# GLA's output projection keeps all its weights on chip, the FFN's norm rows take Ln and Exp, and two steps move in the projections' order

## The chip, the cores and the metric

The kernel runs on one core of one Trainium2 chip. The core has TensorE (PE in the profile, its weight loads PEld), VectorE (DVE), ScalarE (ACT), GpSimd (POOL) and SyncE (SP, which here issues nearly all DMAs). The metric is the device time of one execution in microseconds: 2878.23 us as the median of three runs before the change.

## The reference

One step of an encoder trunk of two layers. 1056 tokens (1024 of a new stream, 32 of a running one), width 1024, all in float32:

```
layer 0: x += Retention(RMSNorm(x));  x += ConvFFN(RMSNorm(x))
layer 1: x += GLA(RMSNorm(x));        x += ConvFFN(RMSNorm(x))
y = RMSNorm(x)

rmsnorm(x, g) = x * rsqrt(mean(x*x) + 1e-6) * g
retention:  ... -> (silu(g) * groupnorm(o)) @ w_out      w_out 2048 x 1024
gla:        ... -> (silu(r) * rmsnorm_head(o)) @ w_out   w_out 1024 x 1024
conv_ffn:   u = h @ w_up (1024 x 5632), causal convolution of width 3,
            silu(gate) * value, @ w_down (2816 x 1024)
```

It also returns the recurrent states of both mixers and the last rows of each convolution.

## The kernel before

**Products.** Activations are held with the width on the 128 partitions and the tokens on the free axis. A float32 product is made of three matmuls: each operand is split into a high half (a cast on ScalarE) and a low half (a subtraction on VectorE, `raw - hi`), and high x high, high x low and low x high are added up in PSUM. A weight of 128 x 1024 is loaded by `load_w` (L99): a DMA of 512 KB into one of three raw slots (L94), the cast and the subtraction of L104 into two of ten "w" tiles (L97) or, for kept weights, into a room of its own ("kw", three pairs).

**The output projections.** The class `Down` (L1211) does retention's (16 k tiles, weights w_ro), GLA's (8 k tiles, w_go) and the last k tiles of each FFN's down projection (6). The first two are named d1 in the code. The tokens are cut into parts: four of 264 for d1, three of 384, 384 and 288 for the FFN. In each part the loop runs over the k tiles; `load` (L1235) brings the weight, unless it is kept from an earlier part, and the part's 264 or 384 columns of the input h, in a raw slot hr of which there are four, and splits them into hh and hl (L1248, L1249; the page calls them XB where they lie in that buffer), of which there are eight each. Each k tile has 8 x 3 matmuls into the eight banks of PSUM (pd, L1273 to L1275). The matmuls of the last k tile go bank by bank, and behind each bank comes its eviction: VectorE adds the residual (L1662 in d1, L1728 in layer 0's down projection), ScalarE squares the result (L138), VectorE and GpSimd add up the squares (L149, L197), and SyncE stores it (L1665).

In parts 1 to 3 the first k tiles are done on seven banks, so that the eighth is free for the norm of the part before: after `hold` k tiles (4 in d1, 3 in the FFN) TensorE sums the squares over the partitions (pn, L201) and `rms_row` (L207 to L212) makes the row 1/rms: mean and epsilon (rm), Sqrt on ScalarE, a reciprocal on VectorE, and one Newton step of three VectorE operations. Then come the eighth bank's matmuls of the steps so far. The work put off to later steps (`done`, `x_sums`) scales the eight tiles by that row (L1678) and makes the sums and splits that the FFN needs (L1339, L1340, L1344). Before the change GLA's d1 keeps k tiles 2 to 4 and loads the other five again in every part; retention's keeps 3 to 5 of 16.

**The FFN's up projection** works in pairs of 128-column blocks by seven products in place of eight. `pair_weights` (L292) makes the seven weights of a pair: two raw loads, rg and rv (L294, L295, in the same three raw slots), and the halves wgh/wgl, wv, wsh/wsl, wth/wtl (L300 to L311, in w tiles). ScalarE and VectorE take the results out of PSUM (pu; L1527 and L1523). The norm of the last part, its scaling and splits are done while the first pair's first products run.

**What sets the order.** The tile framework puts the instructions of each engine into one fixed row when the kernel is built; each engine works through its row in order and waits there on semaphores. Since `run` calls load, matmul and eviction in a certain sequence, the sequence of the code, and the slots of the rooms, decide the rows. `run_tails` (L1201) does four last transposes of retention (pt, from `on`, L831) and their storing, at a chosen place in the following projection.

**Around it.** Layer 1's GLA ends in a gate stage (1966 to 2046 us), which computes silu(r) and multiplies (L1643, L1644); its last weight loads overlap with the first of the projection. The projection follows to 2150 us, then the FFN.

## Time and profile before

| | |
|---|---|
| median of 3 runs | 2878.23 us (2876.97 to 2879.57) |
| profiled execution | 2871.2 us |
| its span | 2869.3 us |
| mean granted TensorE clock | 0.993 |
| TensorE busy | 2791.4 us, 20954 matmuls |
| VectorE busy | 2145.1 us |
| ScalarE busy | 1332.3 us |
| GpSimd busy | 277.8 us |
| retention's projection, layer 0 | 718 to 910 us |
| GLA's projection, layer 1 | 2046 to 2150 us |

The page gives one profiled execution; its time is compared with itself after the change, and the medians with each other. A line such as "PE pd L1274 <- DVE XB L1249: 2.0, 1, 2.0" says that matmuls of line 1274 into pd waited 2.0 us in all, once, 2.0 us the longest, for VectorE's line 1249. A row of the timeline has its start, its length (matmuls are pipelined, so their lengths overlap and the distance of two starts is what one costs), engine, line, operation and tiles, and in brackets the idle time of the engine in front of it with what ended that. PEclk is the granted clock as a share of full speed.

### The profile page before, as it was taken

How to read it: one execution, taken by the hardware profiler on the slowest of the kernel's cores; microseconds unless marked ns; L12 is line 12 of the kernel's file. 1: busy time of each engine (PE TensorE's matmuls, PEld its weight loads, DVE VectorE, ACT ScalarE, POOL GpSimd, SP SyncE). 2: the span in 40 equal slices, each digit the busy share in tenths (PEclk: the TensorE clock that was granted, in tenths of full speed). 3: DMA queues.
4: the chain of work that ended last, by engine and by line, in shares of the span. 5: the costliest groups of instructions: out<-in, count | busy, mean ns of one | idle time of the engine just before them, and what ended most of it. 6: DMA issues, size and time to landing. Idle time of an engine off the chain costs nothing.

```text
span 2869.3 us, 52602 instructions
## 1 busy us (share of the span) xinstructions
PE 2791.4 (97%) x20954; PEld 2687.3 (94%) x20954; DVE 2145.1 (75%) x3529; ACT 1332.3 (46%) x2401; POOL 277.8 (10%) x516
## 2 busy tenths in 40 slices
PE   8999999999999999999999999999998999999998
PEld 8999988788999999999999889999998999999997
DVE  7777777777678887878775577774498788878756
ACT  8433344444444544445443455553254444445434
POOL 1000000000000111111000232220011111110001
PEclk9999999999999999999999999999999999999999
DMA  6333377664765223333867201114642233428663
GB/s 219 106 124 103 128 262 239 199 192 154 260 210 166 82 75 128 121 128 113 286 205 246 90 27 46 51 44 153 222 155 70 75 110 123 143 75 271 210 231 115
DMA packets 234486, 427.22 MB, mean 149 GB/s; under 512 B 27616, under 2 KB 146016, under 8 KB 233216
## 3 DMA queue, kind: packets, MB, share of 16 engines
q1 hardware_dynamic: 233696, 423.27, 44.4%
q8 instruction: 164, 2.69, 0.4%
q14 instruction: 82, 0.67, 0.1%
q10 hardware_dynamic: 544, 0.59, 0.1%
HBM read 299.94 MB, written 123.85 MB: 148 GB/s over the span
## 4 chain that ended last, share of the span: by engine, by line
PE 80%; DVE 9%; DMA 4%; ACT 3%; issue 2%; POOL 1%; SPq 0%; DVEq 0%; ACTq 0%; POOLq 0%
PE pu L333 16%; PE pu L328 16%; PE pu L332 16%; PE pd L1274 3%; PE pd L1275 3%; PE pd L1273 3%; PE psv L233 2%; PE psv L232 2%; PE psv L231 2%; PE pj L124 1%; PE pj L126 1%; PE pj L125 1%; PE pg L124 1%; PE pg L125 1%; PE pg L126 1%
## 5 line engine op out<-in xcount | busy, mean ns | idle before, releaser
L104 DVE TENSOR_TENSOR wlo<-raw,whi 128x1024 fp32r<-128x1024 f32 x161 | 201.3, 1253 | 97.3 <-ACT whi L104 46.0
L1527 ACT COPY AR<-pu 128x264 f32<-128x264 f32 x264 | 99.0, 375 | 303.0 <-PE pu L333 300.3
L104 ACT CAST whi<-raw 128x1024 fp32r<-128x1024 f32 x161 | 167.8, 1047 | 118.4 <-DMA raw<-w_ro 26.7
L333 PE MATMUL pu<-XA,wgl 128*128 128x264 f32 x752 | 213.8, 284 | 0.0
L328 PE MATMUL pu<-XA,wgh 128*128 128x264 f32 x752 | 213.3, 284 | 0.0
L332 PE MATMUL pu<-XA,wgh 128*128 128x264 f32 x752 | 213.2, 283 | 0.0
L1274 PE MATMUL pd<-XB,whi 128*128 128x264 f32 x552 | 158.2, 288 | 2.2 <-DVE XB L1249 2.2
L1549 DVE SCALAR_TENSOR_TENSOR AR<-AR,cw 128x1058 f32<-128x1058 f32 x88 | 115.9, 1318 | 58.5 <-ACT AR L1548 55.9
L1275 PE MATMUL pd<-XB,wlo 128*128 128x264 f32 x552 | 158.3, 288 | 0.0
L1273 PE MATMUL pd<-XB,whi 128*128 128x264 f32 x552 | 154.0, 287 | 0.0
L328 PE MATMUL pu<-XA,wsh 128*128 128x264 f32 x520 | 148.7, 286 | 1.7 <-DVE AR L1523 1.0
L333 PE MATMUL pu<-XA,wsl 128*128 128x264 f32 x520 | 148.6, 286 | 0.8 <-DVE wsl L301 0.8
L332 PE MATMUL pu<-XA,wsh 128*128 128x264 f32 x520 | 147.8, 284 | 0.0
L301 DVE TENSOR_TENSOR wtl<-rv,wth 128x1024 fp32r<-128x1024 f32 x58 | 71.0, 1225 | 101.6 <-ACT wth L300 99.6
L1523 DVE TENSOR_TENSOR AR<-AR,pu 128x264 f32<-128x264 f32 (+2 forms) x440 | 144.6, 368 | 0.0
L328 PEld LDWEIGHTS pu<-XA,wgh 128*128 128x128 f32 x752 | 141.6, 188 | 0.0
L332 PEld LDWEIGHTS pu<-XA,wgh 128*128 128x128 f32 x752 | 141.5, 188 | 0.0
L333 PEld LDWEIGHTS pu<-XA,wgl 128*128 128x128 f32 x752 | 141.4, 188 | 0.0
L328 PE MATMUL pu<-XA,whi 128*128 128x264 f32 x448 | 127.5, 285 | 3.8 <-ACT XA L1418 3.0
L333 PE MATMUL pu<-XA,wlo 128*128 128x264 f32 x448 | 127.3, 286 | 1.5 <-DVE wlo L104 1.5
L332 PE MATMUL pu<-XA,whi 128*128 128x264 f32 x448 | 127.0, 285 | 0.2
L328 PE MATMUL pu<-XA,wth 128*128 128x264 f32 x408 | 116.3, 285 | 0.1
(478 smaller groups left out, 10547.1 us busy)
## 6 DMA issues: line engine op xcount, KB each, us to landing
raw<-w_ro SPq DMA_DIRECT2D x52, 512.0 KB, 4.8
rg<-w_up SPq DMA_DIRECT2D x44, 512.0 KB, 3.6
rv<-w_up SPq DMA_DIRECT2D x44, 512.0 KB, 3.5
scr_h<-AR SPq DMA_DIRECT2D x44, 512.0 KB, 2.7
AR<-scr_x SPq DMA_DIRECT2D x32, 528.0 KB, 4.9
scr_x<-AR SPq DMA_DIRECT2D x32, 528.0 KB, 3.6
raw<-scr_w SPq DMA_DIRECT2D x32, 512.0 KB, 5.2
AR<-scr_h SPq DMA_DIRECT2D x28, 528.0 KB, 4.8
```

The costliest lines, as they stand in the source:

```text
L104: ins = S.copy(hi, raw), V.tensor_tensor(lo, raw, hi.bitcast(F32), op=ALU.subtract)
L124: PE.matmul(ps, hi[:, k], rh, start=kt == 0, stop=False)
L301: V.tensor_tensor(l_, src, h.bitcast(F32), op=ALU.subtract)
L328: mm = PE.matmul(ps, wh[:, k], x[:, 0, kt], start=m in (1, 2, 4, 5) and kt == 0, stop=False, skip_group_check=True)
L332: PE.matmul(ps, wh[:, k], x[:, 1, kt], start=False, stop=False, skip_group_check=True)
L333: mm = PE.matmul(ps, wl[:, k], x[:, 0, kt], start=False, stop=kt == 3, skip_group_check=True)
L1273: PE.matmul(o, w[0][:, k], h[0][:, :n], start=i == 0, stop=False)
L1274: PE.matmul(o, w[0][:, k], h[1][:, :n], start=False, stop=False)
L1275: self.last_mm = PE.matmul(o, w[1][:, k], h[0][:, :n], start=False, stop=i == nk - 1)
L1523: V.tensor_tensor(u[:, d:d + n], t[:, o:o + n], b[:, o:o + n], op=op)
L1527: S.copy(t, b)
L1549: V.scalar_tensor_tensor(cj, uj[:, 1:T + 3], cw[:, nt, 1:2], cj, op0=ALU.mult, op1=ALU.add)
```

## The change

- `rms_row`, for the rows of both d1 (not for the final norm): ScalarE makes Ln of the mean and then Exp of -0.5 times it, which is 1/rms, in place of Sqrt on ScalarE and the reciprocal on VectorE. The table set that holds both is loaded ahead, once a layer: in layer 0 behind retention's last Sqrt, in layer 1 behind the gate's last silu. The Newton step stays.
- GLA's d1 keeps all eight weights: k tiles 2, 3 and 4 in the room "kw", and 0, 1, 5, 6 and 7 in the ten w tiles (`ring`). Its last part takes the k tiles of the ring first.
- `load` issues the DMA of the input h ahead of that of the weight, and `run` calls the load of the next part's first k tile before the last k tile's matmuls and evictions. This holds for all of `Down`.
- `run_tails` is called in part 1, after its second k tile, in place of part 0.

```diff
-        S.activation(t_, m_, AF.Sqrt)
-        V.reciprocal(r_, t_)
+        if logs[0]:
+            for ins in (S.activation(t_, m_, AF.Ln), S.activation(r_, t_, AF.Exp, scale=-0.5)):
+                order(ins, logs[0])
+        else:
+            S.activation(t_, m_, AF.Sqrt)
+            V.reciprocal(r_, t_)
...
-        def __init__(self, nk, wsrc, hsrc, chunks, res, sm, keep, hold, narrow=0):
-            self.narrow = narrow
+        def __init__(self, nk, wsrc, hsrc, chunks, res, sm, keep, hold, narrow=0, ring=()):
+            self.narrow, self.ring = narrow, list(ring)
...
+            hr = self.room("hr")[:, :n]
+            nc.sync.dma_start(hr, self.hsrc(kt)[:, c0:c0 + n])
             if kt not in self.keep:
                 w = load_w(self.wsrc(kt))
             else:
                 if kt not in self.kept:
-                    self.kept[kt] = load_w(self.wsrc(kt), self.room("kw"))
+                    self.kept[kt] = load_w(self.wsrc(kt), None if kt in self.ring else self.room("kw"))
                 w = self.kept[kt]
-            hr = self.room("hr")[:, :n]
-            nc.sync.dma_start(hr, self.hsrc(kt)[:, c0:c0 + n])
...
                     kts = list(keep) + [k for k in kts if k not in keep]
+                    if c == len(self.chunks) - 1:
+                        kts = self.ring + [k for k in kts if k not in self.ring]
...
                     self.load(c, kt)
+                    if i == nk - 1 and c + 1 < len(self.chunks):
+                        self.load(c + 1, (self.ring if c + 2 == len(self.chunks) and self.ring else list(keep))[0])
...
-                        if c == 0 and i == self.narrow:
-                            run_tails(sm)
...
                         for nt in range(KT - 1):
                             mm(i, nt)
+                        if c == 1 and i == 1:
+                            run_tails(sm)
...
             d1 = d1r if l == 0 else Down(ntile, lambda k: io[wo][k], lambda k: scr[k], CQ, scr_x if l else io["xT"], sm,
-                      range(2, 5), 4)
+                      range(8), 4, ring=(0, 1, 5, 6, 7))
             d1.sm = sm
+            logs[0] = S.preload_act_table_set("natural_log_exp_and_others")
+            order(logs[0], last_r[0])
```

The new lines shift the numbers: in the rows of the changed kernel L208 and L215 to L217 are the norm's row, L210 its Ln and Exp, L1253 and L1254 the split of h, L1245 its DMA, L1280 to L1282 the matmuls into pd, L1671 and L1740 the evictions, L299 and L300 the raw loads of `pair_weights`.

More of the change, by code (lines that the diff above doesn't have):

```diff
@@ L158, in trunk_kernel @@
     last_r = [None]
+    logs = [None]
     def rms_a(ss, c, ps, again=False, after=None):
@@ L811, in chunk @@
                             op0=ALU.mult, op1=ALU.add)
-            S.activation(ab[:L, 1:2], ab[:L, 0:1], AF.Sqrt)
+            last_r[0] = S.activation(ab[:L, 1:2], ab[:L, 0:1], AF.Sqrt)
             V.reciprocal(ab[:L, 1:2], ab[:L, 1:2])
@@ L1642, in second @@
             run_tails(sm)
-            S.activation(sg, sg, AF.Silu)
+            last_r[0] = S.activation(sg, sg, AF.Silu)
             V.scalar_tensor_tensor(sg, o, gn[:, f:f + 1], sg, op0=ALU.mult, op1=ALU.mult)
@@ L1716, in second @@
         if last:
+            logs[0] = None
             with pool("db") as dp:
```

## The prediction

> **What bounds the kernel now.** I read the page's busy times and chain first, then the windows of the stage that the change touches most, GLA's output projection in layer 1 (2046 to 2150 us) and the start of the FFN behind it, then what TensorE waited for there.

> ```profile
> PE 2791.4 (97%) x20954; PEld 2687.3 (94%) x20954; DVE 2145.1 (75%) x3529; ACT 1332.3 (46%) x2401; POOL 277.8 (10%) x516
> PE 80%; DVE 9%; DMA 4%; ACT 3%; issue 2%; POOL 1%; SPq 0%; DVEq 0%; ACTq 0%; POOLq 0%
> ```

> TensorE is busy 97% of the span, and the change removes no matmul. So only its waits, and stretches at a lower granted clock, can be won. The windows of the stage give, in order: PE, PEld, DVE, ACT, POOL busy, the granted clock, the DMA share and GB/s.

> ```profile
> 2069.00:2092.00 23.00, 23.00 (x190) 22.93 (x189) 16.63 (x30) 11.22 (x21) 3.56 (x6) 1.00 0.50 158
> 2092.00:2119.00 27.00, 26.28 (x211) 25.68 (x210) 25.82 (x45) 14.17 (x27) 4.50 (x6) 1.00 0.56 184
> 2119.00:2150.00 31.00, 27.12 (x194) 26.64 (x195) 29.72 (x48) 14.44 (x23) 8.23 (x10) 0.90 0.46 151
> 2150.00:2160.00 10.00, 6.02 (x36) 5.51 (x36) 8.70 (x13) 4.80 (x8) 1.84 (x3) 0.84 0.27 87
> 2160.00:2180.00 20.00, 18.05 (x136) 17.23 (x136) 18.68 (x30) 7.28 (x12) 0.00 (x0) 0.98 0.22 71
> ```

> A part of the projection is some 192 matmuls and takes 23 us where TensorE runs alone. The later ones take 27 and 31 us, and there VectorE is busy 25.82 of 27 and 29.72 of 31 us: it is the bound in the third and fourth part and on into the FFN (18.68 of 20). TensorE's waits from 2046 to 2190 us, with the sum, the times and the longest:

> ```profile
> PE pu L328 <- ACT wsh L300: 4.5, 2, 3.9
> PE pd L1274 <- DVE XB L1249: 2.0, 1, 2.0
> PE pn L201 <- POOL ss L197: 1.9, 1, 1.9
> PE pu L328 <- DVE AR L1523: 1.3, 1, 1.3
> PE pu L328 <- ACT AR L1527: 0.9, 1, 0.9
> PE pu L332 <- DVE XB L1340: 0.5, 1, 0.5
> PE pd L1273 <- DVE rm L207: 0.5, 1, 0.5
> PE pd L1273 <- DVE AR L1662: 0.2, 1, 0.2
> ```

> The four on pd and pn, 2.0 + 1.9 + 0.5 + 0.2 = 4.6 us, lie in the projection; the four on pu, 4.5 + 1.3 + 0.9 + 0.5 = 7.2 us, at the start of the FFN. The clock column adds to that: (1 - 0.90) x 31 = 3.1 us in the fourth part, 0.16 x 10 + 0.02 x 20 = 2.0 us after it. In all 16.9 us, which is the most that layer 1 can give. How the clock follows the waits is seen in TensorE's timeline:

> ```profile
> 2129.26 0.71 PE L201 MATMUL pn<-ss,ones 128*128 128x264 f32 x2 [1.90 <-POOL ss L197]
> 2130.29 0.42 PE L1275 MATMUL pd<-XB,wlo 128*128 128x264 f32 x1
> 2130.51 0.42 PE L1274 MATMUL pd<-XB,whi 128*128 128x264 f32 x1
> 2133.89 0.28 PE L1274 MATMUL pd<-XB 128*128 128x264 f32 x1
> 2134.01 0.29 PE L1275 MATMUL pd<-XB 128*128 128x264 f32 x1
> ```

> Behind the wait of 1.90 us a matmul starts every 0.22 us, and some three us later again every 0.12 us: a wait of that size costs nearly as much again in clock.

> **The change part by part.** *GLA's weights kept.* The loads and VectorE's groups in the projection (count | busy, mean ns of one | idle before):

> ```profile
> L102 SPq DMA_DIRECT2D raw<-w_go x23: 328/333/742, 1979.3 to 2133.3; - x23
> L104 DVE TENSOR_TENSOR wlo<-raw,whi 128x1024 fp32r<-128x1024 f32 x16 | 21.1, 1320 | 2.9 <-ACT whi L104 2.9
> L209 DVE RECIPROCAL R<-rt 128x264 f32<-128x264 f32 x3 | 5.4, 1798 | 2.4 <-ACT rt L208 2.4
> L1662 DVE TENSOR_TENSOR AR<-AR,pd 128x264 f32<-128x264 f32 x31 | 11.7, 420 | 0.8 <-PE pd L1275 0.8
> L149 DVE TENSOR_TENSOR ss<-ss,sq 128x264 f32<-128x264 f32 x10 | 4.9, 486 | 1.9 <-ACT sq L138 1.9
> ```

> 23 loads become 8: 15 weight tiles fewer, five in each later part. VectorE's row there, between the end of the second part and the norm of it (wlo is the low half of a w_go tile, XB the split of the projection's input, rm and R the norm's row), was in before:

> ```order
> L149 TENSOR_TENSOR ss_23116<-ss_23116,sq_23421 128x264
> L104 TENSOR_TENSOR wlo_23559<-raw_23556,whi_23558 128x1024
> L1249 TENSOR_TENSOR XB_22807<-AR_22097,XB_22807 128x264
> L104 TENSOR_TENSOR wlo_23605<-raw_23602,whi_23604 128x1024
> L1249 TENSOR_TENSOR XB_22807<-AR_22097,XB_22807 128x264
> L104 TENSOR_TENSOR wlo_23645<-raw_23642,whi_23644 128x1024
> L1249 TENSOR_TENSOR XB_22807<-AR_22097,XB_22807 128x264 x2
> L104 TENSOR_TENSOR wlo_23685<-raw_23682,whi_23684 128x1024
> L207 TENSOR_SCALAR rm_23548<-pn_23545 128x264
> L209 RECIPROCAL R<-rt_23549 128x264
> ```

> And the same place now:

> ```order
> L149 TENSOR_TENSOR ss_23121<-ss_23121,sq_23396 128x264
> L1254 TENSOR_TENSOR XB_22808<-AR_22098,XB_22808 128x264
> L208 TENSOR_SCALAR rm_23514<-pn_23511 128x264
> L215 TENSOR_TENSOR rt_23515<-R 128x264
> L216 SCALAR_TENSOR_TENSOR rt_23515<-rt_23515,rm_23514 128x264
> L1254 TENSOR_TENSOR XB_22808<-AR_22098,XB_22808 128x264
> L217 SCALAR_TENSOR_TENSOR R<-rt_23515,R 128x264
> ```

> The four wlo, and the reciprocal, are gone; nothing took their place. From 2069 to 2150 us VectorE worked 16.63 + 25.82 + 29.72 = 72.2 us. A later part loses 5 x 1.32 = 6.6 us of weights and 1.8 us of reciprocal, three parts 25.2 us. That leaves 47.0 us, and the first FFN weights, which now move into the last part, give back one split of 1.3 us and four half-wide operations of some 0.65, 3.9 us: 51 us for three parts that TensorE needs 3 x 23 us for. VectorE is then no bound in the projection, and I take all 4.6 us of waits and 5.1 us of clock as gone. SyncE, before, near the projection's end (rg and rv are the raw first FFN weights):

> ```order
> L102 DMA raw_23969<-w_go 128x1024
> L1665 DMA scr_x<-AR_22097 128x264 x8
> L1246 DMA AR_22097<-scr_og 128x264
> L1259 DMA AR_22097<-scr_x 128x8x264
> L102 DMA raw_24008<-w_go 128x1024
> L294 DMA rg_24079<-w_up 128x1024
> L295 DMA rv_24080<-w_up 128x1024
> ```

> Now, still in the gate stage ahead of the projection:

> ```order
> L299 DMA rg_23991<-w_up 128x1024
> L1654 DMA scr_og<-AR_22098 128x1056
> L1245 DMA AR_22098<-scr_og 128x264 x2
> L300 DMA rv_23992<-w_up 128x1024
> L1654 DMA scr_og<-AR_22098 128x1056
> L1245 DMA AR_22098<-scr_og 128x264
> L1264 DMA AR_22098<-scr_x 128x8x264
> L1245 DMA AR_22098<-scr_og 128x264
> L299 DMA rg_24045<-w_up 128x1024
> ```

> So the first FFN weights sit on chip a whole stage earlier, and only the tiles for their halves are waited for, which the last part's order (0, 1, 5, 6, 7 first) frees from its fifth step on. Behind the last eviction VectorE still has wsl to make. From the first eviction on it works 8 x 0.42 + 3 x 0.49 + 1.3 = 6.1 us, with a half-wide combine of some 0.6 us (half a wlo) 6.7 us. TensorE has 21 matmuls of the projection left then, and 28 of the FFN before the first that reads wsl: 49 x 0.12 = 5.9 us. A wait of 0.8 us comes out, up to 2.4 if the evictions start late; I take 1.5 of the 4.5 as left. Of the other 2.7 I take 1.1 as gone, by the shorter norm below. So 4.6 + 5.1 + 3.0 + 1.1 = 13.8, less 0.8 for the even chance that the 1.5 us bring back a dip of 1.7: **13.0 us**, between 9 (the wait for the weights stays) and 16.9.

> [...]

> *Ln and Exp for the square root and the reciprocal.* One norm of layer 1 on ACT:

> ```profile
> 2080.97 1.28 ACT L208 ACT_TABLE_LOAD   x1 [8.63 <-DVE rm L207]
> 2082.26 0.43 ACT L208 ACTIVATE rt<-rm 128x264 f32<-128x264 f32 x1
> ```

> and then on VectorE:

> ```profile
> 2082.72 1.80 DVE L209 RECIPROCAL R<-rt 128x264 f32<-128x264 f32 x1 [1.83 <-ACT rt L208]
> ```

> Each of the eight norms loses 1.80 us of VectorE and gains one activation of 0.43 us: 1.4 us less on the chain, 1.8 less on VectorE. Three norms per layer lie beside matmuls; the fourth lies at the FFN's start, and in layer 0, where no weight changes, that is all there is to win:

> ```profile
> 920.00:940.00 20.00, 16.76 (x127) 15.48 (x126) 19.69 (x28) 8.11 (x11) 0.00 (x0) 1.00 0.09 27
> PE pu L328 <- DVE AR L1523: 1.0, 1, 1.0
> PE pu L328 <- ACT AR L1527: 1.0, 1, 1.0
> PE pu L332 <- DVE XB L1340: 0.5, 1, 0.5
> ```

> VectorE, 19.69 of 20 us busy, sets it; of 2.5 us of waits I take **1.6** as gone (0 to 1.8, the reciprocal). The new table load stands, in layer 0, in front of the retention's last normalisation, and in layer 1 behind the gate's last silu instead of on the first norm:

> ```profile
> 713.26 0.77 ACT L826 ACTIVATE on<-po,ab 32x512 f32<-32x512 f32 x1 [1.31 <-DVE ab L815]
> ```

> 1.28 us fit into an idle time of 1.31 us, so it costs nothing; if half of it showed, 0.6 us. [...]

> *Input split ahead of the evictions, input DMA ahead of the weight's.* Where the first layer's projection goes from part 0 to 1 stands this wait:

> ```profile
> PE pt L831 <- DVE AR L1662: 2.9, 1, 2.9
> ```

> It is an eviction queued behind two weight splits that wait for their own DMAs. These stay, so I take **0.4** (0 to 0.6). The four retention transposes (pt) that stood in this wait now run in part 1; that moves their matmuls and removes none. In layer 0's FFN down projection, part 0 to 1, TensorE:

> ```profile
> 1564.72 1.03 PE L1273 MATMUL pd<-hh,ehi 128*128 128x384 f32 x5
> 1568.67 0.90 PE L1273 MATMUL pd<-hh,ehi 128*128 128x384 f32 x2 [2.92 <-DVE AR L1728]
> 1570.07 0.55 PE L1274 MATMUL pd<-hl,ehi 128*128 128x384 f32 x1 [0.50 <-DVE hl L1249]
> ```

> and VectorE's last sum for the norm:

> ```profile
> 1572.96 0.54 DVE L149 TENSOR_TENSOR ss<-ss,sq 128x384 f32<-128x384 f32 x1
> ```

> Before, TensorE's row took seven products of hh, then those of hl:

> ```order
> L1273 MATMUL pd_17090<-hh_17066,ehi_16674 128x384
> L1273 MATMUL pd_17094<-hh_17066,ehi_16674 128x384
> L1274 MATMUL pd_17070<-hl_17067,ehi_16674 128x384
> L1275 MATMUL pd_17070<-hh_17066,elo_16675 128x384
> L1274 MATMUL pd_17074<-hl_17067,ehi_16674 128x384
> ```

> Now all three products of the first k tile go bank by bank, and the norm's pn stands in the second one:

> ```order
> L1281 MATMUL pd_17095<-hl_16989,ehi_16675 128x384
> L1282 MATMUL pd_17095<-hh_16988,elo_16676 128x384
> L1280 MATMUL pd_17071<-hh_17100,ehi_16728 128x384
> L1280 MATMUL pd_17075<-hh_17100,ehi_16728 128x384
> L1280 MATMUL pd_17079<-hh_17100,ehi_16728 128x384
> L1280 MATMUL pd_17083<-hh_17100,ehi_16728 128x384
> L1280 MATMUL pd_17087<-hh_17100,ehi_16728 128x384
> L1280 MATMUL pd_17091<-hh_17100,ehi_16728 128x384
> L1280 MATMUL pd_17095<-hh_17100,ehi_16728 128x384
> L169 MATMUL pn_17151<-ones,ss_16815 128x1
> ```

> hl's wait (0.50) goes, and work fills the wait for the banks (2.92). But pn needs the sum of squares that was done only at 1573.5 us, and TensorE stands there instead. I take **1.0** of the 3.4 us; -0.5 to 2.4.

> Sum: 13.0 + 1.6 + 0.4 + 1.0 = 16.0 us. The profiled execution took 2871.2 us, 1.9 more than its span of 2869.3; 16.0 us are 0.56% of it. The median of the three runs is 7.0 us higher, 2878.23; less 0.56% it is **2862.2 us**. The bounds add to 8.5 and 21.7 us.

> **The rivals.** *The wait for the first FFN weights returns.* Ten w tiles hold five kept weights to the last part, and all four of its first steps free theirs together, after the eighth bank's matmuls. Then four casts and four subtracts (1.3 us) come at once on two engines that also evict. For it: the 4.5 us already there, and VectorE's 8.70 of 10 us. Against: the raw weights wait on chip. It would keep the 4.1 us of the FFN start and, with a dip or two, 3 us of clock: a gain near 8, 2870 us.

> [...]

> *No change.* The waits were for input DMAs all along, so that VectorE's relief buys nothing in the projection: 16.0 - 4.6 - 5.1 - 3.0 leaves 3.3 us, 2875 us. Against it stand VectorE's 29.72 of 31 us.

> *Slower.* In every part the next part's first input split now stands on VectorE ahead of eight evictions. If its DMA has not landed, all eight banks stay full and TensorE stands still: 2.9 us a time by the wait of layer 0, and 1.7 of clock. There are ten such places (three in each projection of a mixer, two in each down projection); from four on, 4 x 4.6 = 18 us, the gain is gone, and at six the kernel takes 2862 + 28 = 2890 us. For it: layer 0's wait of 2.9 us is of this kind, an eviction late in VectorE's row. Against it: the input's DMA moves up too, and SyncE issues it four tiles ahead. That the change doesn't do what it says is excluded by the rows: 8 loads, and one table load a layer.

> **How the numbers follow.** The forecast gets 0.58, the returning wait 0.16, the dips that stay 0.07, no change 0.11, slower 0.08. A measurement of this kernel can tell about 0.2%, 5.8 us, from no change: below 2872.5 us is faster, 0.58 + 0.16 + 0.07 = 0.81; same 0.11; slower 0.08. The range takes in the forecast with its bounds and the first two rivals, 2855 to 2871 us, and leaves out the last two, 0.19.

> **What would show it.** In the changed profile: w_go loaded 8 times; the third and fourth part at about 23 us each with a clock of 1.00; no wait of pd or pn over 0.5 us there; the FFN of layer 1 starting about 8 us earlier against the gate's end; waits of pu at its start near 4 us; the wait at 1568 us replaced by a shorter one of pn. I am wrong if VectorE is still busy over 95% in the fourth part, if pu waits over 4 us for wsh or wsl, or if a wait of 2 us or more on evictions stands at several part ends.

## The result, and the profile after

| | before | changed |
|---|---|---|
| median of 4 runs each, same chip | 2878.9 us (2876.97 to 2886.28) | 2848.96 us (2844.65 to 2849.49) |
| ratio, 95% interval | | 0.9888 [0.9868, 0.9908] |
| the same two programs on another chip | 2873.62 us | 2849.97 us, 0.9909 [0.9894, 0.9924] |
| profiled execution, its span | 2871.2, 2869.3 us | 2849.5, 2847.7 us |

The change makes the kernel faster by 26 to 32 us (0.0091 x 2873.62 and 0.0112 x 2878.9), where 16.0 were forecast; 2848.96 us lies below the range of the forecast. The spans of the two profiled executions differ by 21.6 us. The page of the changed kernel:

```profile
PE 2784.6 (98%) x20954; PEld 2681.9 (94%) x20954; DVE 2109.5 (74%) x3506; ACT 1320.2 (46%) x2395; POOL 278.5 (10%) x516
PE 82%; DVE 7%; DMA 4%; ACT 4%; issue 1%; POOL 1%; SPq 0%; DVEq 0%; ACTq 0%; POOLq 0%
L102 SPq DMA_DIRECT2D raw<-w_go x8: 328/332/432, 1968.3 to 2003.2; - x8
```

The count of matmuls is the same, VectorE has 35.6 us less work, w_go is loaded 8 times. The windows of GLA's projection (now 2035 to 2132 us) and the FFN's start, columns as in the prediction:

```profile
2058.00:2081.00 23.00, 23.00 (x190) 22.93 (x189) 13.80 (x32) 8.05 (x19) 3.68 (x6) 1.00 0.26 80
2081.00:2106.00 25.00, 25.00 (x206) 24.93 (x205) 16.01 (x34) 9.07 (x20) 3.81 (x7) 1.00 0.27 86
2106.00:2132.00 26.00, 24.36 (x200) 24.08 (x199) 23.19 (x41) 11.96 (x23) 7.58 (x8) 1.00 0.27 88
2132.00:2142.00 10.00, 8.40 (x53) 7.88 (x51) 8.38 (x13) 5.01 (x11) 3.00 (x3) 0.83 0.58 198
2142.00:2162.00 20.00, 17.72 (x136) 16.63 (x135) 19.65 (x31) 8.87 (x13) 0.00 (x0) 1.00 0.09 30
```

VectorE's 25.82 of 27 us have become 16.01 of 25, and TensorE has no idle time in these two windows. In the last part VectorE is still busy 23.19 of 26 us, and at the FFN's start 19.65 of 20: there it remains the bound. TensorE's waits from 2035 to 2176 us:

```profile
PE pu L333 <- ACT AR L1536: 1.8, 2, 0.9
PE pd L1280 <- DVE rm L208: 1.6, 1, 1.6
PE pu L338 <- DVE wsl L306: 0.8, 1, 0.8
PE pu L333 <- ACT wth L305: 0.7, 1, 0.7
PE pu L337 <- DVE XB L1349: 0.5, 1, 0.5
```

4.6 us of waits in the projection have become 1.6, 7.2 us at the FFN's start 3.8.

**Where the time came from.** The traces are cut at the same numbers in TensorE's row of matmuls, and a stage is the distance between the starts of two of them. The columns name the layers l0 and l1; "clock" is half the time at clock 0.50 between 100 and 2800 us, which is about what these stretches cost if TensorE works through them: in the one at 2130.04 us before, 3.41 us long, matmuls of 264 columns start 0.22 us apart, behind it 0.12 us, so it costs 1.5 us by its rows and 1.7 us by this count.

| us | l0 projection | l0 FFN start | l0 down, part 0 to 1 | GLA start | l1 projection + FFN start | clock |
|---|---|---|---|---|---|---|
| before | 195.4 | 54.1 | 55.2 | 36.4 | 170.6 | 13.6 |
| before, again | 195.0 | 54.1 | 55.2 | 36.4 | 170.7 | 11.9 |
| changed | 191.2 | 52.9 | 51.0 | 33.1 | 159.8 | 8.5 |
| changed, again | 192.1 | 53.4 | 51.0 | 33.0 | 158.5 | 3.4 |

From the layer-0 projection on, the changed trace is 24.6 us shorter: 4.2 + 1.2 + 4.2 + 3.3 + 10.8, and 0.9 in stages that the change does not touch. Up to 713 us the rows of all engines are the same, and the changed execution happened to be 3.0 us behind (714.02 and 717.04 us at the cut). Two of the five differences stood nowhere near that size in the forecast: 4.2 us in layer 0's down projection (1.0) and 3.3 us at GLA's start (nothing).

### The profile page after: what moved, and what is told of

Same layout as the page of the kernel before. It is cut to its first block, busy times and chain, and to the rows that moved or that the text cites. A ratio compares the mean times of both kernels' runs of the same rounds, so it can differ in the third digit from the quotient of the medians.

```text
span 2847.7 us, 52541 instructions
## 1 busy us (share of the span) xinstructions
PE 2784.6 (98%) x20954; PEld 2681.9 (94%) x20954; DVE 2109.5 (74%) x3506; ACT 1320.2 (46%) x2395; POOL 278.5 (10%) x516
## 4 chain that ended last, share of the span: by engine, by line
PE 82%; DVE 7%; DMA 4%; ACT 4%; issue 1%; POOL 1%; SPq 0%; DVEq 0%; ACTq 0%; POOLq 0%
PE pu L338 16%; PE pu L333 16%; PE pu L337 16%; PE pd L1281 4%; PE pd L1280 4%; PE pd L1282 4%; PE psv L238 2%; PE psv L237 1%; PE psv L236 1%; PE pj L124 1%; PE pj L126 1%; PE pj L125 1%; PE pg L124 1%; PE pg L125 1%; PE pg L126 1%
## 5 line engine op out<-in xcount | busy, mean ns | idle before, releaser
L104 DVE TENSOR_TENSOR wlo<-raw,whi 128x1024 fp32r<-128x1024 f32 x146 | 180.7, 1241 | 100.9 <-ACT whi L104 44.9
L104 ACT CAST whi<-raw 128x1024 fp32r<-128x1024 f32 x146 | 152.3, 1048 | 110.7 <-DMA raw<-w_ro 38.0
L1280 PE MATMUL pd<-XB,whi 128*128 128x264 f32 x552 | 157.9, 286 | 1.6 <-DVE rm L208 1.6
L1282 PE MATMUL pd<-XB,wlo 128*128 128x264 f32 x552 | 157.0, 284 | 0.0
L1281 PE MATMUL pd<-XB,whi 128*128 128x264 f32 x552 | 156.7, 284 | 0.0
```

The costliest lines, as they stand in the source:

```text
L104: ins = S.copy(hi, raw), V.tensor_tensor(lo, raw, hi.bitcast(F32), op=ALU.subtract)
L1280: PE.matmul(o, w[0][:, k], h[0][:, :n], start=i == 0, stop=False)
L1281: PE.matmul(o, w[0][:, k], h[1][:, :n], start=False, stop=False)
L1282: self.last_mm = PE.matmul(o, w[1][:, k], h[0][:, :n], start=False, stop=i == nk - 1)
```

## The experiments

**Each part undone.** Four kernels are the changed one without one part.

```diff
# u_weights
-                      range(8), 4, ring=(0, 1, 5, 6, 7))
+                      range(2, 5), 4)
# u_lnexp
-            logs[0] = S.preload_act_table_set("natural_log_exp_and_others")
-            order(logs[0], last_r[0])
# u_ahead: hr's DMA behind the weight's again, and
-                    if i == nk - 1 and c + 1 < len(self.chunks):
-                        self.load(c + 1, ...)
# u_tails: run_tails(sm) in part 0 again
```

> The changed kernel with GLA's projection keeping k tiles 2 to 4 again (23 loads of w_go in place of 8), the rest of the change as it is. Theory by the two traces: between the start of the projection of layer 1 and the FFN behind it 10.8 us were won, most of it by the weights; without them 7 to 10 us come back, a time near 2857 us (0.992 to 0.993 of the kernel before), with VectorE busy over 93% in the fourth part. Rival: the shorter norm row (Ln and Exp) already frees VectorE enough; then at most 3 us come back, under 2852 us.

> The changed kernel with Sqrt and the reciprocal in all norm rows and no table load ahead. Theory: each norm at an FFN's start costs 1 to 2 us more, and the wait for rm late in layer 0's projection (1.24 us before, gone now) returns: 4 to 5 us, near 2853 us. Rival: the norm rows lie beside matmuls everywhere, and the wait for rm went by the input loads; then under 1.5 us.

> The changed kernel with the weight's DMA ahead of the input's again and without the early load of the next part's first k tile. Theory: the wait of 2.9 us and the half-clock stretch between part 0 and 1 of layer 0's down projection return (4.2 us), and so does the wait of 3.4 us for the last evictions at the start of GLA, since it is the order of the down projection's matmuls that decides which bank is free for GLA's first product: 8 to 9 us, near 2858 us. Rival: GLA's start does not hang on this but on the transposes moved in layer 0; then the down projection alone returns, 4 us, near 2853 us.

> The changed kernel with retention's last transposes in part 0 again. Theory: nothing is removed by that move, within 1.5 us of the changed kernel, 2848 to 2851 us, and GLA's start keeps its new shape. Rival: the move shifts the order in which the eight banks are taken from then on; then the wait of 3.4 us at GLA's start returns, near 2853 us.

> The changed kernel once more, as a base for the others on the same chip and as a second trace of the same program. Theory: the instructions are the same on every engine up to 713 us and differences there between profiles are chance; the half-clock stretches behind short waits come and go from run to run. Expected 0.987 to 0.991 of the kernel before, with the first 700 us moved by up to 3 us against the first trace. Rival: the first 700 us repeat within 0.5 us, so that the change does something there.

Measured, with the stages of each trace:

| without | median us | ratio | l0 down | GLA start | l1 projection + FFN start |
|---|---|---|---|---|---|
| kept weights | 2859.07 | 0.9951 [0.9936, 0.9966] | 51.0 | 33.1 | 166.0 |
| Ln and Exp | 2855.95 | 0.9935 [0.9922, 0.9948] | 51.0 | 33.1 | 164.0 |
| split ahead | 2853.23 | 0.9926 [0.9912, 0.9940] | 55.2 | 33.1 | 160.1 |
| tails in part 1 | 2857.73 | 0.9939 [0.9926, 0.9952] | 51.0 | 37.6 | 158.9 |
| nothing (changed, again) | 2849.97 | 0.9909 [0.9894, 0.9924] | 51.0 | 33.0 | 158.5 |

Each ratio is against the kernel before on the same chip (medians of 2873.5 to 2876.1 us on the four chips used), so the medians of different chips are not compared with each other. Undoing any part costs something. The interval of the split ahead overlaps that of the whole, and that of Ln and Exp just touches it; there the stages decide. Without the split ahead 55.2 us come back at just the place, and without Ln and Exp the last stage is 164.0 us. GLA's start hangs on the transposes of retention, some 850 us ahead of it, and on no other part.

**Each part alone**, put into the kernel before, and that kernel once more as a control:

> The kernel before with nothing but retention's last transposes moved from part 0 to part 1 of its projection. Theory: the transposes no longer take a bank in part 0, the order in which the eight banks go round shifts, and bank 0, which GLA's first product needs, belongs to the fifth and not to the seventh eviction of the down projection; the wait of 3.4 us at GLA's start is gone, 3 to 4 us (0.9985 to 0.999), more where a half-clock stretch goes with it. Rival: it needs the early load too; then under 1 us.

> The kernel before with Ln and Exp in the rows of both projections and nothing else. Theory: in layer 1, where VectorE is the bound from the third part on, four reciprocals of 1.8 us count nearly whole, and in layer 0 the waits at the FFN's start fall by 1 us and the wait of 1.2 us for rm may go: 5 to 9 us (0.997 to 0.998). Rival: only the norm at each FFN's start counts; 2 to 4 us.

> The kernel before with all eight w_go weights kept and the ring first in the last part, and nothing else. Theory: with Sqrt and the reciprocal left in, the projection of layer 1 and the FFN's start behind it (170.6 us before) take 164 us, as they do in the kernel that lacks Ln and Exp: 6 to 7 us, 0.9975 of the kernel before, with no half-clock stretch in the projection. Rival: the weights need the shorter norm as well; under 3 us.

> The kernel before with the input's DMA first and the early load of the next part's first k tile, and nothing else. Theory: the down projection of layer 0 gains its 4.2 us, GLA's start keeps its wait of 3.4 us: 4 us, 0.9985 of the kernel before. If the four parts alone add up to the whole (6.5 + 5 + 6 + 4 = 21 to 22 us against the 26 of the second measurement), the change is a plain sum. Rival: the early load holds up evictions in the other projections, 0 or slower.

> The kernel before once more, as a second trace of the same program. Theory: its times agree with the kernel before within 0.1%, its waits repeat, but its half-clock stretches do not: they cost 13.7 us in the first trace, and 4 to 16 us is expected, in the projections, behind GLA's start wait or inside GLA. Rival: the same stretches at the same places.

| alone | median us | ratio | stage it changes, us |
|---|---|---|---|
| tails in part 1 | 2868.09 | 0.9976 [0.9968, 0.9985] | GLA start 36.4 to 33.1 |
| Ln and Exp | 2869.67 | 0.9975 [0.9964, 0.9986] | l0 FFN start 54.1 to 52.9; layer 1 170.6 to 166.0 |
| kept weights | 2869.45 | 0.9979 [0.9968, 0.9989] | layer 1 170.6 to 165.0 |
| split ahead | 2871.36 | 0.9984 [0.9974, 0.9995] | l0 down 55.2 to 51.0 |
| nothing (before, again) | 2873.95 | 1.0002 [0.9990, 1.0014] | none |

The four gains add to 0.86% (24.7 us of 2873.62), and the whole gives 0.91%: within the noise the parts add up. (The four losses of the table before add to 1.15%, as far off on the other side.) Their stages add to 3.3 + 1.2 + 4.6 + 5.6 + 4.2 = 18.9 us.

**Why the transposes matter to GLA's start.** Before, the timelines of VectorE and TensorE there (pj is GLA's first product; the row of L1728 x3 holds the evictions six to eight):

```profile
1619.40 0.45 DVE L1728 TENSOR_TENSOR AR<-AR,pd 128x288 f32<-128x288 f32 x1
...
1622.33 1.17 DVE L1728 TENSOR_TENSOR AR<-AR,pd 128x288 f32<-128x288 f32 x3
...
1619.47 0.29 PE L1275 MATMUL pd<-hh,kl 128*128 128x288 f32 x1
1623.19 0.44 PE L124 MATMUL pj<-XA,whi 128*128 128x384 f32 x1 [3.42 <-DVE AR L1728]
```

The changed kernel:

```profile
1611.96 0.45 DVE L1740 TENSOR_TENSOR AR<-AR,pd 128x288 f32<-128x288 f32 x1
...
1614.91 1.17 DVE L1740 TENSOR_TENSOR AR<-AR,pd 128x288 f32<-128x288 f32 x3
...
1612.03 0.29 PE L1282 MATMUL pd<-hh,kl 128*128 128x288 f32 x1
1612.46 0.45 PE L124 MATMUL pj<-XA,whi 128*128 128x384 f32 x1
```

Now pj starts when the fifth eviction ends (1611.96 + 0.45 = 1612.41). Before, it stood until the seventh was done, the second of the three (a start every 0.37 us, the last two 0.44 long: 1622.33 + 0.37 + 0.44 = 1623.14). With the transposes alone moved, and with them alone moved back:

```profile
1619.32 0.45 PE L124 MATMUL pj<-XA,whi 128*128 128x384 f32 x1
```

```profile
1613.40 0.69 PE L124 MATMUL pj<-XA,whi 128*128 128x384 f32 x1 [3.43 <-DVE AR L1740]
```

The reason can be read in the built programs, which name the bank of every tile (the traces do not). GLA's first pj takes bank 0 of PSUM in both. The tiles of a projection take the eight banks in rotation; in part 0 the pt tile of the transposes takes a turn, in part 1 it has the spare eighth bank. So the rotation is shifted by one, and layers later the seven banks of the last part lie as 1, 4, 5, 2, 0, 7, 6 in place of 1, 4, 5, 2, 7, 6, 0: bank 0 is the fifth that is evicted, not the seventh.

**What of the split ahead does it.** One half of that edit each, and then the norm's matmul put behind the third k tile:

```diff
# u_next (no early load)
-                    if i == nk - 1 and c + 1 < len(self.chunks):
-                        self.load(c + 1, ...)
# u_hfirst (hr's DMA behind the weight's again)
# pn_late
-    lambda c, ss: rms_a(ss, c, sm("pn")), ...
+    lambda c, ss: rms_a(ss, c, sm("pn"), after=down.last_mm), ...
```

> The changed kernel without the early load of the next part's first k tile; the input's DMA still goes ahead of the weight's. Theory: the early split alone makes the down projection's first k tile go bank by bank, so its wait of 2.9 us and the half-clock stretch return, 4 us, near 2853 us. Rival: the order of the two DMAs did it; under 1 us.

> The changed kernel with the weight's DMA ahead of the input's; the early load of the next part's first k tile stays. Theory: nothing waits for that order where it counts, within 1.5 us of the changed kernel. Rival: the down projection's gain hangs on it, 4 us more.

> The changed kernel with the sum over partitions (pn) of layer 0's down projection held back behind the third k tile, in place of standing in the second one. Theory: the 1.15 us that TensorE still waits for the sum of squares there go, and nothing else is late: about 1 us less than the changed kernel, 2847 to 2850 us. Rival: the norm comes so late that the eighth bank waits for it; the same or 1 to 2 us more.

Without the early load (2850.79 us, 0.9914 [0.9897, 0.9930]) TensorE's two waits of before are back:

```profile
1565.34 0.90 PE L1280 MATMUL pd<-hh,ehi 128*128 128x384 f32 x2 [2.92 <-DVE AR L1738]
1566.74 0.54 PE L1281 MATMUL pd<-hl,ehi 128*128 128x384 f32 x1 [0.49 <-DVE hl L1254]
```

Without the other half (2850.58 us, 0.9909 [0.9892, 0.9925]) nothing changes against the changed kernel, whose only wait there is the first row below; the second fence is pn_late's (2853.06 us, 0.9914 [0.9898, 0.9929]):

```profile
1567.62 0.38 PE L169 MATMUL pn<-ones,ss 128*128 128x1 f32 x2 [1.15 <-DVE ss L149]
```

```profile
1565.22 0.45 PE L1281 MATMUL pd<-hl,ehi 128*128 128x384 f32 x1 [1.61 <-DVE hl L1254]
```

So the load ahead of the evictions is worth 4.2 us in its stage, the order of the DMAs nothing that can be seen, and moving pn back does not win its wait: the next one, on hl, is 1.61 us. The times of u_next and u_hfirst can't be told apart from the whole; that 4.2 us belong to the early load is shown by the stages (55.2, 51.0 and, with it alone undone, 55.2).

**Kept weights or VectorE's row.** The forecast gave the ring's order a role. plain_ring takes the last part's k tiles in the order 0 to 7:

```diff
-                    if c == len(self.chunks) - 1:
-                        kts = self.ring + [k for k in kts if k not in self.ring]
```

> The changed kernel with the last part of GLA's projection in the order 0 to 7, so that the ten tiles held by k tiles 5, 6 and 7 are freed only at its end. Theory: the first FFN weights wait for these tiles, 3 to 6 us more at the FFN's start, near 2852 us. Rival: four of the five ring weights are freed together behind the eighth bank's matmuls anyway, and the order matters under 1.5 us.

2848.37 us, 0.9910 [0.9896, 0.9924], layer 1 in 158.5 us: no effect of the order can be seen. Three of its waits there:

```profile
PE pd L1278 <- DVE rm L208: 1.7, 1, 1.7
PE pu L338 <- DVE wsl L306: 0.8, 1, 0.8
PE pu L333 <- ACT wth L305: 0.8, 1, 0.8
```

With the kept weights alone (only_weights), where w_go is also loaded 8 times and the ring's order is the changed kernel's:

```profile
PE pu L328 <- ACT wth L300: 1.9, 1, 1.9
PE pd L1275 <- DVE rm L207: 1.9, 1, 1.9
PE pu L328 <- DVE AR L1525: 1.3, 1, 1.3
PE pu L328 <- ACT wsh L300: 0.6, 1, 0.6
```

The waits of pu at the FFN's start fall only from 7.2 to 6.3 us (the rows not shown are under 1 us each). With Ln and Exp alone (only_lnexp) TensorE's three largest waits, the one on pd still in the projection, are these:

```profile
PE pu L338 <- DVE wgl L306: 3.3, 1, 3.3
PE pd L1279 <- DVE XB L1254: 2.2, 1, 2.2
PE pu L333 <- DVE AR L1528: 1.9, 2, 1.3
```

wsh is waited for 0.7 us in place of 4.5, but wgl, a low half that VectorE makes, 3.3 us, and the waits of pu add to 7.4 us. In the changed kernel they are 3.8; without its kept weights they are 7.5, without its Ln and Exp 6.8. So at the FFN's start the waits go only when both parts are there. That each part alone still wins about half of the stage (5.6 and 4.6 us of 10.8 to 12.1) comes from the projection, whose waits of 4.6 us fall to 2.1 and 2.4, and from one half-clock stretch fewer. Both parts shorten VectorE's row, and the tile that is waited for changes with them; that this length is the cause fits all these traces, but no run changes it alone.

What remains in the projection is the wait of 1.6 us for rm. Whether a later norm would remove it stays open: the one variant made for that (hold 5 in place of 4) does not compute the same function, and no time of it is used here.

## Why the prediction was right in direction and wrong in size, step by step

**The two sums side by side.** Of the forecast's 16.0 us, 4.3 were clock (5.1 - 0.8) and 11.7 the rest. The gain of the second measurement can be divided in the same way, since the mean granted clock is on record for every timed execution. On that chip it was 0.9922 in the mean of 17 executions of before and 0.9960 in that of four of the changed kernel. Counting (1 - clock) x span as lost, these lost 22.5 and 11.4 us: 11 us of the gain are clock (about 1 us either way), and 14 (about 2 either way) are the rest. So the term that was missed by most is the clock: the forecast took 5.1 us of it from the stretches beside the waits of layer 1 in one trace, and the loss fell by 11. In the rest, the moved transposes were put at nothing and gave 3.3 us, and the split ahead gave 2.5 us and 1.7 of clock for 1.0. None of the signs of being wrong that the forecast named appeared (VectorE is busy 23.19 of 26 us in the last part's window, which is 89%): the miss lay where it did not look.

**GLA's projection and the FFN's start, 13.0 us: about right in sum, 10.8 and 12.1 measured, its division wrong.** Of the 4.6 us of waits in the projection 3.0 went, not all: one of 1.6 us, where the eighth bank's matmuls wait for the norm's mean (rm), took their place. Counted in matmuls (192 of pd and two of pn a part), the four parts took 23.5, 23.8, 24.7 and 31.4 us before and take 23.5, 23.8, 23.8 and 25.6 us now, where about 23 had been said for the last two. So the third part had only 1 us to give: the 27 us read for it are the length of a window of 211 matmuls, more than one part. The FFN began 6.8 us earlier against the gate's end, where 8 had been said (projection 2046.13 to 2149.54 and 2035.12 to 2131.74 us). The waits at the FFN's start are 3.8 us for "near 4" (the forecast's own terms, 7.2 - 3.0 - 1.1, leave 3.1), and the 1.5 us left for the weights' halves came out (wsl 0.8, wth 0.7). But the step "the last part's order (0, 1, 5, 6, 7 first) frees from its fifth step on" the tiles that wsh needs is not what won them: no effect of the order was seen, and the 3.0 us set down for the kept weights and the 1.1 for the shorter norm come only together (6.3 us of waits with the weights alone, 7.4 with Ln and Exp alone). The rival of the returning wait for the first weights is out, and so is the one in which the waits were for the inputs' DMAs. For the dips that stay, 0.07 of the chances, no run shows a ground: in the changed trace the projection's waits are 1.6 us in place of 4.6, and the clock is 1.00 in the third and fourth part, where the fourth had 0.90.

**Ln and Exp.** Layer 0's FFN start: 1.6 us forecast, 1.2 and 0.7 measured, and 1.2 with that part alone. In layer 1 it is worth 4.6 us alone, where 1.1 were set down for it at the FFN's start; the sum of the stage had the rest under the weights. The new table load of 1.28 us costs nothing that the rows show, as said. ScalarE's rows at the end of retention, changed:

```profile
714.72 0.20 ACT L817 ACTIVATE ab<-ab 32x1 f32<-32x1 f32 x1 [3.15 <-DVE ab L815]
714.94 1.28 ACT L1699 ACT_TABLE_LOAD   x1
716.24 0.77 ACT L831 ACTIVATE on<-po,ab 32x512 f32<-32x512 f32 x1
```

The load takes the place of the idle time of 1.31 us ahead of the last normalisation, which follows it at once.

**The split ahead in layer 0's down projection: 1.0 forecast, 4.2 measured.** The step that failed: "But pn needs the sum of squares that was done only at 1573.5 us, and TensorE stands there instead." It held VectorE's row fixed. That row before, from the first evictions on (the last sum into ss, at 1572.96, stands in the prediction):

```profile
1561.28 1.59 DVE L1728 TENSOR_TENSOR AR<-AR,pd 128x384 f32<-128x384 f32 x3 [3.28 <-PE pd L1275]
...
1568.07 1.47 DVE L1728 TENSOR_TENSOR AR<-AR,pd 128x384 f32<-128x384 f32 x3
1569.46 0.55 DVE L1249 TENSOR_TENSOR hl<-AR,hh 128x384 fp32r<-128x384 f32 x1
...
1571.21 0.55 DVE L1249 TENSOR_TENSOR hl<-AR,hh 128x384 fp32r<-128x384 f32 x1
```

And now:

```profile
1558.02 1.59 DVE L1740 TENSOR_TENSOR AR<-AR,pd 128x384 f32<-128x384 f32 x3 [2.02 <-PE pd L1282]
...
1562.64 1.47 DVE L1740 TENSOR_TENSOR AR<-AR,pd 128x384 f32<-128x384 f32 x3
...
1567.02 0.55 DVE L149 TENSOR_TENSOR ss<-ss,sq 128x384 f32<-128x384 f32 x1
1567.49 1.01 DVE L1254 TENSOR_TENSOR hl<-AR,hh 128x384 fp32r<-128x384 f32 x2
```

The sixth and seventh of the eight evictions came 6.8 and 7.3 us behind the first one (the three at 1568.07 are the sixth to eighth) and now come 5.1 and 5.6 us behind it (the three at 1562.64 are the fifth to seventh), the two splits (hl) that stood ahead of the last sum now stand behind it, and ss is done 9.6 us after the first eviction began (1558.02 to 1567.57), not 12.2 (1561.28 to 1573.50). So pn waits only 1.15 us; of 3.4 us of waits 2.3 are gone, within the bound of 2.4. On top of that the stretch at clock 0.50 that stood behind the wait of 2.92 us is gone, 1.7 us, which the forecast did not count here; it stands in all seven traces that have this wait and in none of the nine that don't.

**The transposes: nothing forecast, 3.3 us measured.** The step that failed is "That moves their matmuls and removes none": it is true, and misses that a tile also holds a place in the rotation of PSUM's banks. The wait of 3.42 us at GLA's start was not in the forecast's list of waits at all, since no line of the diff touches that place. This is the term that was left out.

**The layer-0 projection, part 0 to 1: 0.4 forecast, not settled.** The wait there is chance. In before it was 2.89 and 4.74 us in two executions of one program, in the changed one 1.90 and 2.98, and in plain_ring, whose row there is the same as the changed kernel's:

```profile
763.98 0.51 PE L1278 MATMUL pd<-XB 128*128 128x264 f32 x1 [5.16 <-DVE AR L1669]
```

The stage took between 189.9 and 195.4 us over all traces; it is 194.7 us in the mean of the six with the transposes in part 0 and 192.6 in that of the ten with them in part 1, but the two groups overlap, and the wait varies by as much within one program. A gain of 2 us is likely by these means and not shown.

**The slower rival** is out: of its ten places only layer 0's projection, part 0 to 1, has a wait on an eviction of near 2 us or more in the changed traces (1.9 and 3.0), and it had one before; layer 0's down projection, another of them, became shorter.

**What is left over** is clock. Without their half-clock stretches (one fewer in layer 0's down projection, two fewer in layer 1) the four stages that the change surely shortens give 1.2 + 2.5 + 3.3 + 7.4 = 14.4 us, which agrees with the 14 us of the timed executions; the 11 us of clock come on top. The parts alone divide them so: against before on the same chip the loss fell by 4.1 us with the kept weights, 3.6 with the transposes, 2.0 with the split ahead and 1.3 with Ln and Exp, each uncertain by 1 to 2 us, together 11.0. The forecast counted the clock only where it saw stretches beside the waits it took away. In six traces of programs that are before or before with one part the clock lost 11.9 to 22.2 us (only_weights the most), in the changed program and plain_ring 8.5, 3.4 and 1.7, and in the kernels that lack a part or half of one 3.4 to 13.7. Two traces with the same waits at GLA's start show how it varies. Before, and below it before with the kept weights alone, 95 us from the wait on:

```profile
1613.00:1708.00 95.00, 86.55 (x665) 80.22 (x663) 70.67 (x146) 51.65 (x149) 28.77 (x37) 1.00 0.14 47
```

```profile
1612.00:1707.00 95.00, 88.25 (x632) 82.39 (x631) 68.48 (x144) 50.10 (x144) 28.19 (x37) 0.91 0.14 47
```

Nothing in the diff of only_weights touches this stage, and the granted clock is 0.91 for 1.00, (1 - 0.91) x 95 = 8.6 us. Three of the six traces with the wait of 3.4 us have such a group of stretches from there on, each 8.5 us of loss by GLA's end; the ten traces without that wait lost 0 to 5.1 us in GLA. The profiled execution of before was one without it, and its 2871.2 us lie 7.7 us under the median of 2878.9. That the executions of before lose more clock is shown by their records; that it is these waits which bring it on in them is argued from the traces, since the records of the timed executions hold one mean clock and no places.

## What to carry to other kernels

Before a change is costed, list the trace's long waits, also where no edited line stands, and ask of each moved tile which bank or slot it takes from whom: a step that costs TensorE nothing can shift a rotation and decide a wait (of 3.4 us here) some 850 us later. When a term is "work that fills a wait, until the next wait", shift the whole row of the engine that is waited for before pricing the next wait. And price a wait with the clock that may fall behind it as a chance, not as what one trace shows: it was there in some executions of a program and not in others (13.6 and 11.9 us of clock in two of before, 8.5 and 3.4 in two of the changed kernel). Where the mean clock of each execution is on record, divide the gain into clock and the rest before explaining it.
